# New durations in a schedule planner, constants moved into shared buffers, and 42 slots of SBUF

## The chip, the cores and the metric

The kernel runs on one core of a Trainium2 chip. The metric is the device time of one launch in microseconds; the time before is the median of three runs. TensorE is called PE here, VectorE DVE, ScalarE ACT, GpSimdE POOL, and SyncE SP; SP issues all DMAs of this kernel.

## What is computed

Two layers over 256 tokens of width 1024. Each layer is a gated feed-forward block, a mixer, and another feed-forward block, each with a residual and a layer norm. The mixer of layer 0 joins a gated delta rule (8 heads) with an mLSTM (4 heads); that of layer 1 is a state space mixer (SSD, 32 heads in 4 groups).

```python
def reference(x, ...):
    for l in range(DEPTH):                       # DEPTH = 2
        x = _layer_norm(DN_ALPHA * x + 0.5 * _swiglu(x, ffn_pre_w_gate[l], ffn_pre_w_up[l], ffn_pre_w_down[l]), ...)
        mix = _hybrid_mixer(x, ...) if l % 2 == 0 else _ssd_mixer(x, ...)
        x = _layer_norm(DN_ALPHA * x + mix, ...)
        x = _layer_norm(DN_ALPHA * x + 0.5 * _swiglu(x, ffn_post_w_gate[l], ...), ...)
    return x

def _swiglu(x, w_gate, w_up, w_down):
    return (jax.nn.silu(x @ w_gate) * (x @ w_up)) @ w_down

def _gated_delta_rule(q, k, v, g, beta):         # chunks of the sequence
    ...
    lower = jnp.where(strict, jnp.einsum('bhncd,bhnjd->bhncj', kb, k) * decay, 0.0)
    sol = lax.linalg.triangular_solve(lower + jnp.eye(CHUNK), rhs, left_side=True, lower=True)
    ...
```

## The kernel before, in words

All weights are fp32. A weight tile is loaded in two halves of 512 KB into `raw`; ACT rounds it to `hi`, DVE computes `lo = raw - hi`, and PE multiplies with three products (`mm3`: hi by hi, hi by lo, lo by hi). `wget` keeps `AHEAD` = 4 weights in flight. The feed-forward stages make `gu` (gate and up), then `sg` (Silu on ACT), `hf` (product on DVE), and accumulate the down product in `acc`.

The hybrid mixer (`hyb`) runs token-major products (`tm_chunks`), then the gates of both heads as rows (`softplus`, scans against a tile of ones, a transposition through scratch memory in HBM), the convolutions of k, the matrices `Ls` of the delta rule, and the inverse of its 16 x 16 diagonal blocks (`block_inverse`, all on DVE). The blocks reach the inverse through scratch memory: `Ls` is written to `scrdl`, two loads of 64 KB bring `ab` (pieces of 16 floats), and the results go out through `scrdd` and come back as `T` and `U` for level matmuls of PE. In the meantime the mLSTM part multiplies `mq` and `mk` into `mE`, then `mE` by `mv1`; DVE makes `my` of it, and PE transposes `my`. After it come the convolutions of q and v (`conv_in`: a product in `acc`, ACT's scaled copy `cv` of the PSUM bank, three DVE operations on the same bank, a Silu).

The SSD mixer (`ssd`) has token-major products for `zs`, a softplus and scans, `decays` (a load `abc` of rows from scratch, 8 relus with a bias on ACT and an exponential for each group and half), convolutions for B (`bf`), C (`cf`) and x (`xf`), and `chunk`: `xd`, `xe` and `y` from a transposition, the state `hst` copied by ACT, products `gu`, a normalization, and transpositions into `syh` and `syl`.

The order of the work is not written by hand. Each call is recorded as an `Op` in a `Plan`. `_cost` gives it a duration, `rank` a due time counted backwards from the PE order, and `order` simulates the engines: at each step it takes for each engine the operation with the smallest priority among those that can start (SP and PE never wait for a better one, the others do for a short time), until every queue is fixed. Operations under `hp()` count as 600 places earlier. `behind(op)` says that an operation is placed only after another has been placed. What `order` believes decides only the order; on the chip each engine runs its queue in that order and waits on semaphores. Buffers come from tags with a fixed number of slots (`SB_SLOTS`): `m4` is the large one, for weights and for the mixers' tiles, then `m2`, `m1` and two tiny ones; PSUM has 8 banks. A DMA in the plan ended at max(queue, issue) + bytes/rate + 2000 ns, and 1000 more for `raw`.

Of the kernel before, what the change touches and what calls it, by code (L numbers as in the profile page):

```python
# [19 lines left out]
P = 128  # L20
D = 1024
S = 256
# [10 lines left out]
NSLOT = 40  # L33
# [7 lines left out]
C_EYE16 = 896  # L41
C_LOW16 = 1152
C_N = 1408


def _const_array():
# [9 lines left out]
    c[:, C_LOW16:C_LOW16 + 256] = np.tril(np.ones((16, 16), np.float32), -1).reshape(1, 256)  # L56
    c[:, C_EYE16:C_EYE16 + 256] = np.eye(16, dtype=np.float32).reshape(1, 256)
# [3 lines left out]
SB_SLOTS = {"m4": (NSLOT, WMAX), "m2": (6, 512), "m1": (6, 256), "tiny": (12, 16), "tiny96": (12, 96)}  # L61
# [12 lines left out]
class Buf:  # L74


    def __init__(self, n, tag, shape, dtype, name):
# [6 lines left out]
        self.ops = []  # L84
        self.place = None
# [99 lines left out]
class Plan:  # L185
# [83 lines left out]
    def _cost(self, op, method, a, k):  # L269
# [12 lines left out]
        elif q == "SP":  # L282
# [5 lines left out]
            op.rate = 410 if isinstance(src, bass.AP) and not src.tensor.name.startswith("scr") else 300  # L288
        else:
# [20 lines left out]
            elif q == "ACT":  # L310
                op.busy += 180 + .85 * n + 60 * scal - LAG["ACT"] + (186 if "accum_out" in k else 0)
# [38 lines left out]
    MARGIN, LEAD = 1000, 0  # L350
# [3 lines left out]
    def order(self):  # L354
# [18 lines left out]
        dma = 0.0  # L373
# [12 lines left out]

        def start(o, q):
            t = max(ready[o, q], clock[q])
            if o.news:
# [23 lines left out]
        while len(out) < len(ops):  # L413
            best = None
            for q in QUEUES:
# [4 lines left out]
                now = [(o.prio + 2 * switch(o, q), o.n, t, o) for t, o in can if t <= t0]  # L420
                mine = min(now)
                for p, n, t, o in sorted((o.prio + 2 * switch(o, q), o.n, t, o) for t, o in can if t > t0):

                    if p + self.WAIT * (t - t0) < mine[0] and t - t0 < self.FRAC[q] * mine[3].busy:
                        mine = (p, n, t, o)
                        break
# [20 lines left out]
            if q == "SP":  # L447
                first = max(dma, t + busy)
                dma = first + max(350, o.bytes / o.rate)
                end = dma + 2000 + self.MARGIN * o.raw  # L450
# [6 lines left out]
            o.done, o.begun, o.on = end, t, q  # L457
            out.append(o)
# [32 lines left out]
class Net:  # L491
# [92 lines left out]
    def consts(self):  # L584
# [7 lines left out]
        self.ones = self.one([32, S], F32, name="ones")  # L592
        nc.gpsimd.memset(self.ones, 1.0)
# [277 lines left out]
    def hyb(self, g, b, last=False):  # L871
# [24 lines left out]
        ones = self.ones[0:8]  # L896

# [38 lines left out]
        with hp():  # L936
            sin = t96(12, "sin")
            V.tensor_copy(sin[:, :, 0:8], gt[:, :, 8:16])
            V.tensor_scalar_mul(sin[:, :, 8:12], gt[:, :, 20:24], -1.0)
# [15 lines left out]
            rw = self.m4([8, 4, S], nm="hrows")  # L955
            for half in range(2):
# [130 lines left out]
        mq = self.m4([P, 2, S], nm="mq")  # L1087
# [3 lines left out]
        mk = self.m4([P, 2, S], nm="mk")  # L1091
# [3 lines left out]
        for pr in range(2):  # L1095
            for q in range(2):
# [5 lines left out]
                qk = V.tensor_mul(e, e, ps[:, 0:3 * P])  # L1102
        with hp():
# [533 lines left out]
```

## Time and profile before

| | us |
|---|---|
| median of three runs (1146.54 to 1148.89) | 1147.33 |
| the profiled execution, whole | 1146.67 |
| its span, first to last instruction | 1144.9 |
| PE busy | 1112.7 |
| DVE busy | 758.5 |
| ACT busy | 587.9 |

The mean granted clock of PE is 0.995 of full speed. The feed-forward stages lie at about 0 to 200, 380 to 560, 560 to 750 and 960 to 1145 us, the hybrid mixer at 200 to 380, and the SSD mixer at 750 to 960. Matmuls overlap in PE, so one shows a longer duration (281 ns for 256 columns) than the distance to the next. A row of the list of waits names the waiting engine and tile, the one waited for, us in total, how often, and the longest.

### The profile page before, as it was taken

The page shows a single profiled execution, that of the slowest core. Times are in us where ns is not written, and L with a number is a line of the kernel's source. Part 1 is how long each engine was busy: PE and PEld are TensorE (multiplying, and loading weights), DVE is VectorE, ACT ScalarE, POOL GpSimd, SP SyncE. Part 2 cuts the span into 40 slices and gives each one's busy share as a digit, 9 for nine tenths or more (in the row PEclk, how much of TensorE's full clock was granted, in tenths as well). Part 3 has the DMA queues.
Part 4 walks back from the last instruction along what each step waited for, and adds up shares of the span by engine and source line. Part 5 has one row for each costly group of instructions (what it writes and reads, how often), then busy time and mean ns, then how long its engine had stood idle before and what let it go on. Part 6 is the DMA issues. An engine that isn't in the chain of part 4 may idle for free.

```text
span 1144.9 us, 19783 instructions
## 1 busy us (share of the span) xinstructions
PE 1112.7 (97%) x8118; PEld 1041.5 (91%) x8118; DVE 758.5 (66%) x1242; ACT 587.9 (51%) x890; POOL 26.2 (2%) x53
## 2 busy tenths in 40 slices
PE   7999999998999999999999999999999999999996
PEld 7999998998998999999899999899998779999995
DVE  6945456787969955455865545696788889655425
ACT  6755443593423544344354444379889636444410
POOL 0000000000000000000000000000011220000000
PEclk9999999998999999999999999999999999999999
DMA  9766554648424555565465555465545446655601
GB/s 358 288 212 205 196 183 133 191 171 214 186 102 159 197 190 192 191 206 174 148 223 200 188 197 187 134 217 187 185 146 178 149 163 243 218 172 187 212 19 37
DMA packets 75955, 210.02 MB, mean 183 GB/s; under 512 B 13580, under 2 KB 26328, under 8 KB 75864
## 3 DMA queue, kind: packets, MB, share of 16 engines
q1 hardware_dynamic: 75864, 208.76, 54.3%
q8 instruction: 63, 1.03, 0.4%
q14 instruction: 28, 0.23, 0.1%
HBM read 204.23 MB, written 4.50 MB: 182 GB/s over the span
## 4 chain that ended last, share of the span: by engine, by line
PE 81%; DVE 8%; ACT 6%; DMA 3%; issue 1%; SPq 0%; DVEq 0%; ACTq 0%
PE gu L488 46%; PE acc L488 32%; PE tr L488 3%; DVE cv L488 2%; DMA raw<-in_wgu 2%; DVE lo L488 2%; ACT L488 2%; ACT abc L488 1%; DVE x L488 1%; ACT cv L488 1%; DMA ab<-scrdl 1%; ACT Ls L488 1%; ACT hi L488 0%; DVE ry L488 0%; DMA x<-in_x 0%
## 5 line engine op out<-in xcount | busy, mean ns | idle before, releaser
L488 DVE TENSOR_TENSOR lo<-raw,hi 128x1024 fp32r<-128x1024 f32 (+2 forms) x358 | 428.8, 1216 | 145.0 <-ACT hi L488 141.4
L488 ACT CAST hi<-raw 128x1024 fp32r<-128x1024 f32 (+2 forms) x358 | 370.1, 1045 | 203.0 <-DMA raw<-in_wgu 125.1
L488 PE MATMUL gu<-xl,hi 128*128 128x256 f32 x1216 | 341.9, 281 | 0.0
L488 PE MATMUL gu<-xh,hi 128*128 128x256 f32 x1216 | 341.2, 281 | 0.0
L488 PE MATMUL gu<-xh,lo 128*128 128x256 f32 x1216 | 341.1, 281 | 0.0
L488 PEld LDWEIGHTS gu<-xh,hi 128*128 128x128 f32 x1216 | 229.0, 188 | 1.0
L488 PEld LDWEIGHTS gu<-xl,hi 128*128 128x128 f32 x1216 | 228.9, 188 | 1.1
L488 PEld LDWEIGHTS gu<-xh,lo 128*128 128x128 f32 x1216 | 229.1, 188 | 0.0
L488 PE MATMUL acc<-hi,h 128*128 128x512 f32 (+1 forms) x748 | 228.7, 381 | 0.0
L488 PEld LDWEIGHTS acc<-hi,h 128*128 128x128 f32 x748 | 138.1, 188 | 27.5
L488 PE MATMUL acc<-lo,h 128*128 128x512 f32 (+1 forms) x374 | 142.1, 380 | 0.0
L488 ACT ACTIVATE sg<-gu 128x256 f32<-128x256 f32 (+1 forms) x100 | 35.9, 359 | 183.3 <-PE gu L488 183.1
L488 DVE TENSOR_TENSOR hf<-sg,gu 128x256 f32<-128x256 f32 (+1 forms) x100 | 38.7, 388 | 108.2 <-ACT sg L488 108.0
L488 PE MATMUL acc<-xh,hi 128*128 128x256 f32 x320 | 92.7, 290 | 0.0
L488 PE MATMUL acc<-xl,hi 128*128 128x256 f32 x320 | 90.5, 283 | 0.0
L488 PE MATMUL acc<-xh,lo 128*128 128x256 f32 x320 | 90.2, 282 | 0.0
L488 PEld LDWEIGHTS acc<-lo,h 128*128 128x128 f32 x374 | 70.3, 188 | 13.1
L488 PE MATMUL acc<-hi,xh 128*128 128x260 f32 x224 | 64.0, 286 | 0.0
L488 PE MATMUL acc<-hi,xl 128*128 128x260 f32 x224 | 63.4, 283 | 0.4 <-DVE xl L488 0.4
L488 PE MATMUL acc<-lo,xh 128*128 128x260 f32 x224 | 63.3, 283 | 0.0
L488 PEld LDWEIGHTS acc<-xh,hi 128*128 128x128 f32 x320 | 61.0, 190 | 0.6 <-issue 0.2
L488 DVE TENSOR_TENSOR h<-hf,h 128x256 fp32r<-128x256 f32 x76 | 32.3, 425 | 44.0 <-ACT h L488 44.0
(272 smaller groups left out, 1445.5 us busy)
## 6 DMA issues: line engine op xcount, KB each, us to landing
raw<-in_wgu SPq DMA_DIRECT2D x176, 512.0 KB, 5.0
raw<-in_wd SPq DMA_DIRECT2D x88, 512.0 KB, 5.8
raw<-in_ssd_fm SPq DMA_DIRECT2D x24, 512.0 KB, 5.7
raw<-in_ssd_tm SPq DMA_DIRECT2D x16, 520.0 KB, 4.5
raw<-in_hyb_fm SPq DMA_DIRECT2D x16, 512.0 KB, 5.2
raw<-in_ssd_out SPq DMA_DIRECT2D x16, 512.0 KB, 5.7
raw<-in_hyb_tm SPq DMA_DIRECT2D x12, 520.0 KB, 4.4
raw<-in_hyb_out SPq DMA_DIRECT2D x8, 512.0 KB, 6.8
```

Source lines behind the costliest of these rows:

```text
L488: getattr(engines[o.on], method)(*map(real, a), **{x: real(v) for x, v in k.items()})
```

## The change

The planner's numbers: a DMA that reads or writes scratch memory in pieces of up to 64 bytes counts 82 bytes/ns, other scratch writes 228 and reads 291 (300 before); DMAs end at the later of issue + 2100 + bytes/rate and the end of the one before + bytes/rate, with 1300 ns more for the second large one of a row, and `LATE` = 200 on top; `MARGIN`, now used by `rank` alone, is 1500. An operation that touches a PSUM bank starts in the plan only when every other engine's last operation on that bank has ended. An ACT operation with a per-partition scalar that reads no PSUM counts 40 ns more. The switching penalty gets a name, `SWITCH` = 2, its value before.

Memory: `m4` has 42 slots instead of 40. The 16 x 16 constants leave `cst` (1408 to 896 columns) for an input of their own, `cst16`, that is loaded into an `m2` slot (`c16`) behind the last `qk`. The tile of ones, set once at the start, becomes two `m1` tiles, set on POOL behind `neg` in the hybrid mixer and behind `soft` in the SSD mixer. `mq` and `mk` share one `m4` slot. `tiny96` has 11 slots of 64.

```diff
@@ -30,7 +30,7 @@
...
 WMAX = KB * CW
-NSLOT = 40
+NSLOT = 42
 RSQRT_MAGIC = 0x5F3759DF
@@ -38,9 +38,7 @@
...
 C_PAIR = 768
-C_EYE16 = 896
-C_LOW16 = 1152
-C_N = 1408
+C_N = 896
@@ -53,12 +51,16 @@
...
     c[:, C_CAU:C_CAU + P] = i <= j
-    c[:, C_LOW16:C_LOW16 + 256] = np.tril(np.ones((16, 16), np.float32), -1).reshape(1, 256)
-    c[:, C_EYE16:C_EYE16 + 256] = np.eye(16, dtype=np.float32).reshape(1, 256)
     return c
...
-SB_SLOTS = {"m4": (NSLOT, WMAX), "m2": (6, 512), "m1": (6, 256), "tiny": (12, 16), "tiny96": (12, 96)}
+def _const16():
+
+    c = np.stack([np.eye(16, dtype=np.float32), np.tril(np.ones((16, 16), np.float32), -1)])
+    return np.broadcast_to(c.reshape(1, 512), (P, 512)).copy()
+
+
+SB_SLOTS = {"m4": (NSLOT, WMAX), "m2": (6, 512), "m1": (6, 256), "tiny": (12, 16), "tiny96": (11, 64)}
 PS_SLOTS = {"ps": 8}
@@ -82,6 +84,7 @@
...
         self.ops = []
+        self.seen = {}
         self.place = None
@@ -285,7 +288,10 @@
...
             op.raw = "raw" in getattr(getattr(out, "buf", None), "name", "")
-            op.rate = 410 if isinstance(src, bass.AP) and not src.tensor.name.startswith("scr") else 300
+            far = [v for v in (out, src) if isinstance(v, bass.AP)][0]
+            if far.tensor.name.startswith("scr"):
+                piece = 4 * far.ap[-1][1]
+                op.rate = 82 if piece <= 64 else 228 if isinstance(src, View) else 291
         else:
@@ -308,7 +314,7 @@
...
             elif q == "ACT":
-                op.busy += 180 + .85 * n + 60 * scal - LAG["ACT"] + (186 if "accum_out" in k else 0)
+                op.busy += 180 + .85 * n + 60 * scal - LAG["ACT"] + (40 if scal and not ps else 0) + (186 if "accum_out" in k else 0)
                 f = a[2] if method == "activation" and len(a) > 2 else None
@@ -347,7 +353,8 @@
...
     PE_DUE = False
-    MARGIN, LEAD = 1000, 0
+    SWITCH = 2
+    MARGIN, LATE, LEAD = 1500, 200, 0
     WAIT = 2
@@ -370,7 +377,7 @@
...
         clock["SP"] = 700.0
-        dma = 0.0
+        dma, row = 0.0, 0
         table = None
@@ -384,8 +391,17 @@
...
+        for o in ops:
+            o.banks = list({v.buf for _, a, k in o.calls for v in list(a) + list(k.values())
+                            if isinstance(v, View) and v.buf.psum})
+
         def start(o, q):
             t = max(ready[o, q], clock[q])
+            for b in o.banks:
+
+                for e, end in b.seen.items():
+                    if e != q:
+                        t = max(t, end + HAND[e][q])
             if o.news:
@@ -417,9 +433,9 @@
...
                 t0 = max(min(t for t, _ in can), clock[q] + 1)
-                now = [(o.prio + 2 * switch(o, q), o.n, t, o) for t, o in can if t <= t0]
+                now = [(o.prio + self.SWITCH * switch(o, q), o.n, t, o) for t, o in can if t <= t0]
                 mine = min(now)
-                for p, n, t, o in sorted((o.prio + 2 * switch(o, q), o.n, t, o) for t, o in can if t > t0):
+                for p, n, t, o in sorted((o.prio + self.SWITCH * switch(o, q), o.n, t, o) for t, o in can if t > t0):
@@ -445,9 +461,10 @@
...
             if q == "SP":
-                first = max(dma, t + busy)
-                dma = first + max(350, o.bytes / o.rate)
-                end = dma + 2000 + self.MARGIN * o.raw
+                took = max(350, o.bytes / o.rate)
+                row = 1 if t + busy >= dma else row + 1
+                dma = max(t + busy + 2100 + took, dma + took + (1300 if row == 2 and took > 900 else 0))
+                end = dma + self.LATE
             if q == "ACT" and o.exps is not None:
@@ -455,6 +472,8 @@
...
             o.done, o.begun, o.on = end, t, q
+            for b in o.banks:
+                b.seen[q] = end
             out.append(o)
@@ -589,8 +608,6 @@
...
         self.x = self.one([P, 2, D], F32, name="x")
-        self.ones = self.one([32, S], F32, name="ones")
-        nc.gpsimd.memset(self.ones, 1.0)
         self.mhalf = self.one([P, 1], F32, name="mhalf")
@@ -893,8 +910,6 @@
...
             DQ(al, self.ap["gdn_a_log"].partition_broadcast(P))
-        ones = self.ones[0:8]
-
         gt = self.one([P, 2, 24], F32, name="hgate")
@@ -936,7 +951,7 @@
...
             V.tensor_copy(sin[:, :, 0:8], gt[:, :, 8:16])
-            V.tensor_scalar_mul(sin[:, :, 8:12], gt[:, :, 20:24], -1.0)
+            neg = V.tensor_scalar_mul(sin[:, :, 8:12], gt[:, :, 20:24], -1.0)
             beta = t96(8, "beta")
@@ -953,6 +968,9 @@
...
             rw = self.m4([8, 4, S], nm="hrows")
+            ones = self.m1([8, S], nm="ones")
+            with self.plan.behind(neg):
+                G.memset(ones, 1.0)
             for half in range(2):
@@ -1084,11 +1102,12 @@
...
-        mq = self.m4([P, 2, S], nm="mq")
+        mqk = self.m4([P, 4, S], nm="mqk")
+        mq = mqk[:, 0:2]
         ps = self.acc()
...
         A.copy(flat(mq), ps)
-        mk = self.m4([P, 2, S], nm="mk")
+        mk = mqk[:, 2:4]
         ps = self.acc()
@@ -1100,8 +1119,11 @@
...
                 qk = V.tensor_mul(e, e, ps[:, 0:3 * P])
+        c16 = self.m2([P, 512], nm="c16")
+        with self.plan.behind(qk):
+            DQ(c16, self.ap["cst16"])
         with hp():
-            self.block_inverse(ab, c, dd)
+            self.block_inverse(ab, c16, dd)
         lazy["sg"] = sg = self.m4([P, 2, 512], nm="sg")
@@ -1285,8 +1307,8 @@
...
         ti = self.m1([P, 16, 16], nm="ti")
-        eye3 = c[:, C_EYE16:C_EYE16 + 256].rearrange("p (a b) -> p a b", a=16)
-        V.tensor_mul(ab, ab, c[:, C_LOW16:C_LOW16 + 256].rearrange("p (a b) -> p a b", a=16))
+        eye3 = c[:, 0:256].rearrange("p (a b) -> p a b", a=16)
+        V.tensor_mul(ab, ab, c[:, 256:512].rearrange("p (a b) -> p a b", a=16))
         V.tensor_sub(an, eye3, ab)
@@ -1362,7 +1384,6 @@
...
             DQ(vec, self.ap["ssd_vec"].partition_broadcast(P))
-        ones = self.ones[:, 0:P]
         t32 = lambda n, nm: self.one([P, n, NH], F32, name=nm)
@@ -1388,7 +1409,7 @@
...
         sp = self.softplus(flat(sdt), 2 * NH)
-        V.tensor_copy(flat(dt), sp)
+        soft = V.tensor_copy(flat(dt), sp)
         nega = t32(1, "snega")
@@ -1397,6 +1418,9 @@
...
         rw = self.m1([NH, S], nm="srow")
+        ones = self.m1([NH, P], nm="ones")
+        with self.plan.behind(soft):
+            G.memset(ones, 1.0)
         ds_ = [self.scratch([NH, P], f"ds{half}") for half in range(2)]
@@ -1574,7 +1598,7 @@
...
     f = lambda a: np.ascontiguousarray(np.asarray(a))
-    o = {"cst": _const_array(), "ident": np.eye(P, dtype=np.float32), "x": f(i["x"])[0]}
+    o = {"cst": _const_array(), "cst16": _const16(), "ident": np.eye(P, dtype=np.float32), "x": f(i["x"])[0]}
     gu, dn = [], []
```

## Rows read from the trace of the kernel before

**Rows 1.** The page's part 1: busy us, share of the span, instructions.

```profile
PE 1112.7 (97%) x8118; PEld 1041.5 (91%) x8118; DVE 758.5 (66%) x1242; ACT 587.9 (51%) x890; POOL 26.2 (2%) x53
```

**Rows 2.** Whom PE waited for: us in total, times, longest us.

```profile
PE tr L488 <- DMA x<-in_x: 5.2, 1, 5.2
PE tr L488 <- DVE my L488: 4.5, 1, 4.5
PE gu L488 <- DVE xe L488: 2.7, 2, 1.7
PE gu L488 <- ACT hst L488: 2.7, 3, 1.9
PE tr L488 <- ACT cf L488: 1.8, 2, 1.5
```

**Rows 3.** One window of 20 us: length, busy us by engine, granted clock, DMA.

```profile
860.00:880.00 20.00, 18.49 (x144) 17.15 (x144) 17.23 (x27) 18.62 (x29) 4.23 (x10) 1.00 0.42 143
```

**Rows 4.** Windows of 2 us around PE's longest stall.

```profile
274.00:276.00 2.00, 2.00 (x10) 2.00 (x11) 1.17 (x7) 0.00 (x0) 0.00 (x0) 0.50 0.85 90
276.00:278.00 2.00, 2.00 (x11) 2.00 (x10) 1.22 (x6) 0.59 (x1) 0.00 (x0) 0.50 0.83 209
278.00:280.00 2.00, 2.00 (x16) 2.00 (x14) 1.97 (x5) 0.00 (x0) 0.00 (x0) 0.71 1.15 327
```

**Rows 5.** Timeline of PE: start, us, what, count [idle before and releaser].

```profile
267.47 1.95 PE L488 MATMUL tr<-mv,mE 128*128 128x129 f32 x16
273.91 0.45 PE L488 MATMUL tr<-ident,my 128*128 128x128 f32 x1 [4.49 <-DVE my L488]
...
301.09 1.05 PE L488 MATMUL gu<-U,Ls 128*128 128x128 f32 x8
```

**Rows 6.** Timeline of DVE in the hybrid mixer.

```profile
259.66 2.35 DVE L488 TENSOR_TENSOR lo<-raw,hi 128x1024 fp32r<-128x1024 f32 x2
264.26 0.43 DVE L488 TENSOR_TENSOR ab<-ab,cst 128x256 f32<-128x256 f32 x1 [2.25 <-DMA ab<-scrdl]
...
273.41 0.61 DVE L488 SCALAR_TENSOR_TENSOR my<-tr,md,sg 128x128 f32<-128x128 f32 x2
```

**Rows 7.** Timeline of SP's DMA issues in the hybrid mixer.

```profile
256.45 0.73 SPq L488 DMA_DIRECT2D ab<-scrdl  x1
...
277.85 1.48 SPq L488 DMA_DIRECT2D T<-scrdd  x1
```

**Rows 8.** DMA issues: count, KB each, median us from issue to landing.

```profile
raw<-in_wgu SPq DMA_DIRECT2D x176, 512.0 KB, 5.0
...
T<-scrdd SPq DMA_DIRECT2D x2, 512.0 KB, 8.3
...
snw<-in_ssd_norm_w SPq DMA_DIRECT2D x4, 256.0 KB, 3.9
...
ab<-scrdl SPq DMA_DIRECT2D x2, 64.0 KB, 6.4
```

**Rows 9.** Chain that ended last: start, us, what.

```profile
40.81 11.37 PE gu L488 x96
```

**Rows 10.** Timelines of ACT and DVE at one convolution of the SSD mixer.

```profile
790.33 0.55 ACT L488 ACTIVATE cv<-acc,scw 128x256 f32<-128x256 f32 x1
...
790.91 0.48 DVE L488 SCALAR_TENSOR_TENSOR cv<-acc,scw,cv 128x255 f32<-128x255 f32 x1 [2.19 <-ACT cv L488]
```

**Rows 11.** Groups of ACT by shape: count, busy us, mean ns.

```profile
L488 ACT ACT_TABLE_LOAD x38 | 48.8, 1283 | 3.4 <-DVE cv L488 2.1 <-PEq L1626 0.7
...
L488 ACT ACTIVATE abc<-abc,spam 128x128 f32<-128x128 f32 x64 | 20.2, 392 | 0.7 <-DVE sde L488 0.7
```

**Rows 12.** Timelines of ACT and PE at a stall in the SSD mixer.

```profile
832.16 1.06 ACT L488 ACTIVATE abc<-abc 128x1024 f32<-128x1024 f32 x1
833.12 0.57 ACT L488 COPY hst<-gu 128x512 f32<-128x512 f32 x1
...
833.74 1.12 PE L488 MATMUL gu<-hst,cf 128*128 128x512 f32 x2 [1.92 <-ACT hst L488]
```

## The prediction

> **What bounds the kernel now.** I read the engine totals first, then who TensorE (PE) waited for, then the same waits by stretch. PE is busy 97% of the span, 1112.7 us of 1144.9 [rows 1]; no instruction of PE is removed by the change, so it can win only among the 32.2 us in which PE stands still, and in time in which PE runs at the lower clock. The waits of PE show where the idle time lies [rows 2]: 5.2 us for the first load of x, which nothing can hide, and then single stalls in the two mixers: 4.5 us for `my` in the hybrid mixer, and 2.7 (`xe`), 2.7 (`hst`) and 1.8 us (`cf`) in the SSD mixer, 7.2 us together. The reader is to see that each of them is one to three places, and that, behind the first load, none of these is a load of weights. A window of 20 us from the SSD mixer shows the other kind [rows 3]: PE loses 1.5 us at full clock, beside an ACT that is busy for 18.6 of 20 us.
>
> The largest stall costs more than its length. Behind it, in pieces of 2 us [rows 4], the granted clock is 0.50 for 4 us (the level of 1.2 GHz) and 0.71 over the next two, in which it comes back to 2.4: 2 x 0.5 + 2 x 0.5 + 2 x 0.29 = 2.6 us lost on top of 4.5. So this one place costs 7.1 us, 0.6% of the kernel. The 1.5 us that PE loses in rows 3 leave the clock at 1.00.
>
> **Why it stalls.** The order is made by `Plan.order`, which guesses when each operation ends and then fixes every queue. PE finishes `tr<-mv,mE` at about 269.4 (267.47 + 1.95) and next has `tr<-ident,my`, which begins at 273.91 [rows 5]. On DVE [rows 6] the load `ab<-scrdl` makes the block inverse start at 264.26, after DVE had been free since 262.01 (259.66 + 2.35); the inverse runs from there with `my` queued behind it, which begins at 273.41. The second `ab` load is issued at 256.45 [rows 7] and is awaited until 264.26, 7.8 us; the median of both is 6.4 us [rows 8]. The plan of before gives such a load 0.33 us of issue, 0.35 of transfer and 2.0 of latency, 2.7 us, so it expects the inverse, and `my`, far too early. Meanwhile `lo` of the next two weights is done at 262.01, so PE could have run the q convolution's 96 matmuls; 96 matmuls take 11.37 us [rows 9], more than twice the stall.
>
> **The change part by part.**
> 1. *Rates of small loads.* `op.rate` falls from 300 to 82 bytes/ns for pieces of up to 64 bytes, so each 64 KB `ab` load now takes 0.80 instead of 0.35 us in the plan. The write of `Ls` (512 byte pieces) goes from 1.75 to 2.30 us each, and the second of a row gets 1.3 us more. Following the plan's own formula along the queue (two `Ls` writes, three weight loads of 1.28 us, two `ab` loads) the second `ab` comes some 2.2 us later in the plan than it did. These are the plan's beliefs, used for the order alone, and not times of the kernel. If `my` comes 2.2 us later there, PE finds other ready matmuls first: at 11.37/96 = 0.118 us each and groups of six, about three groups. At the least 2.2 us of the stall goes and, if the 2.3 us that remain leave the clock alone, as the 1.5 us in rows 3 do, the clock's 2.6 us too: 4.8 us. At the most the whole 7.1 goes. The correction is made in the plan alone, so DVE is not faster; PE's later users of `my` are the output products far behind. I take 6.0.
>
>    A page speaks against this term: the Trainium skill, "DMA: Bandwidth & Descriptors", section "Anatomy of one DMA", gives about 2.0 us fixed plus bytes over 436 GB/s; that is 2.15 us (an estimate from this page) for 64 KB, near the old plan, and by it the correction would be wrong and the term nothing. The trace has 6.4 us for the load, and the measurement decides.
>
> 2. *One reader per PSUM bank.* The plan now lets no second engine at a bank before the first is done. The trace has that order already [rows 10]: ACT reads a bank from 790.33 to 790.88, and DVE, which needs `cv` of it, begins at 790.91 after 2.19 us without work. One pair of rows cannot show the bank alone as the cause. The rule removes nothing from the chip; it makes the convolutions of the plan longer, so that PE is given other work ahead of their consumers (`cf`, 1.8 us).
>
> 3. *Relu with bias.* The plan counts 40 ns more for each of the 64 `abc` relus, 2.6 us of ACT's work in the SSD mixer, and 16 in the hybrid; the trace has 392 ns for one [rows 11], where the old formula says 349. Parts 2 and 3 aim at `hst`, `xe` and `cf`. `hst` is put in ACT's queue behind an exponential at 832.16 and begins at 833.12; PE's `gu<-hst` follows at 833.74 [rows 12]. These stalls come from an ACT that is nearly full there, not from one wrong number, so later guesses cure only those for which PE has other work. Bounds: all 7.2 us gained, or as much lost if the new order makes them worse. I take a quarter, 1.8, nearest to the `cf` stall, the one that hangs on the convolution itself.
>
> 4. *Loads of weights.* The plan now lands a lone 512 KB load 0.7 us sooner and wants it 0.5 us earlier (MARGIN 1500), and there are 42 slots, less one slot in the hybrid since `mq` and `mk` share one. A `wgu` load takes 5.0 us from issue to landing in the trace, with what is queued ahead of it [rows 8], where the plan now has 0.33 + 1.28 + 2.1 + 0.2 = 3.9 for a lone one. PE waits for no load of weights, so nothing is gained; what hides the 1.1 us of difference is the four weights that `wget` keeps ahead. If that cover were gone, 1.1 us would be lost at each of six stage starts, 6.6 us. I take 0.
>
> 5. *Constants.* `cst` shrinks by 256 KB and `c16` brings 256 KB: bytes are the same, one DMA is added. `c16` is queued on SP behind the last product with `mE`, so it comes out near the `ab` loads, and the block inverse waits for both. Its nearest row is `snw`, 256 KB, 3.9 us to landing [rows 8], shorter than `ab`'s 6.4; but the weight loads queued behind it on SP come one issue later (0.4 to 0.7 us), and its data takes part of `ab`'s bandwidth. So the inverse may start 0 to 2 us later. What waits for the inverse is the scratch copy into `T` and `U`: the second `T` is issued at 277.85 [rows 7] with a landing of 8.3 us [rows 8], so about 286, and PE's first product with `U` begins at 301.09 [rows 5]: cover of some 15 us. While `my` stands behind the inverse, though, 2 us would go into the stall. I take 0.5 against the change.
>
> 6. *Memsets.* The 1.0s are set on POOL in the mixers, 256 and 128 columns each; POOL is busy 2% [rows 1]. They stand behind `neg` and `soft` in the plan, and DVE's scans wait for them; what hides them is the softplus on DVE between. POOL's 53 instructions take 0.5 us on the mean (26.2/53). I take nothing; 0.5 us each if uncovered. The `ones` memset at the start goes: nothing, as x's load is awaited.
>
> Sum: -6.0 - 1.8 + 0.5 = -7.3 us. Against the profiled execution's 1146.67 (its span and 1.8 us around it) that is 1139.4; the median shown is 0.7 us above that execution, so 1140.1, and I write 1140.0.
>
> **The rivals.**
> - *The stall stays in place.* The plan's `my` moves, but not beyond the end of `tr<-mv,mE`, or the inverse goes first once more. Then 7.1 us stay, parts 2 and 3 bring 1.8 and part 5 takes 0 to 2: 1145.5 to 1147.5. For it: PE takes the oldest ready operation, and `my` is older than the q convolution. Against: 96 matmuls are ready, and 2.2 us is many groups.
> - *A new stall in the SSD mixer, slower.* There ACT does table loads of 1.28 us for single short operations (38 in all, 48.8 us [rows 11]). If the new order puts one more pair of them and an exponential, 2 x 1.28 + 1.06 = 3.6 us, ahead of `hst` in two of the four groups, the stall of 1.9 becomes 5.5 us, above the 4.5 us that brought the lower clock, with 2.6 us more: 2 x (3.6 + 2.6) = 12.4. With the gain of 6 that is 1147.3 - 6 + 12.4 = 1153.7. It decides from a stall of about 4.5 us. For it: ACT is 93% busy in 860:880. Against: the plan now counts ACT's work more nearly as it is, and the penalty on switching is unchanged.
> - *More goes.* All of the 7.1 and two thirds of the 7.2: 1147.3 - 7.1 - 4.8 = 1135.4.
>
> **How the numbers follow.** Forecast 0.50, more goes 0.19, stall stays 0.15, new stall 0.16. About 0.2% (2.3 us) is what a measurement of this kernel can tell from no change: below 1145.0 is faster, above 1149.6 slower. The forecast and the better case give faster 0.69 and the new stall 0.16; what is left, 0.15, is the same. The range reaches from 1132 (nearly all of 7.1 and 7.2 gained, which would be 1133, and 1 us for the scatter) to 1149 (the stall in place with the 2 us of part 5, 1147.5, and a late memset and a late load, 0.5 + 1.1), and leaves out the slower case.
>
> **What the profile would show.** Right: PE's longest wait after the first load is below 2.5 us; no piece of the hybrid mixer shows a granted clock under 0.9; `acc<-xh,hi` stands ahead of the last `tr<-ident,my`. Part 3 right: the waits for `hst`, `xe` and `cf` sum to about 5.4 us. Wrong: a wait of over 4 us on `hst` or `xe`, more than 38 table loads, or `ab` and `c16` landing after 266 with `my` behind them.

## The result, and the profile after

The changed kernel takes 1133.98 us in the median of four runs (1133.38 to 1135.16) against 1147.77 us of the kernel before on the same chip: a ratio of 0.9881 with a 95% interval of [0.9864, 0.9898], so 13.7 us faster (11.7 to 15.6). The forecast was 1140.0 us with a range of 1132 to 1149. The sign held and the time is in the range, but the gain is nearly twice the 7.3 us of the sum and is nearest to the rival "more goes" (1135.4).

The profiled execution of the changed kernel took 1135.16 us, its span is 1133.4, so the two profiled executions differ by 11.5 us. PE's busy time has hardly moved [rows 1]; the page's part 1:

```profile
PE 1109.6 (98%) x8118; PEld 1039.1 (92%) x8118; DVE 757.2 (67%) x1242; ACT 585.9 (52%) x886; POOL 24.0 (2%) x54
```

Whom PE waited for in the changed kernel (us in total, times, longest):

```profile
PE tr L507 <- DMA x<-in_x: 5.0, 2, 4.7
PE gu L507 <- DVE xe L507: 2.7, 3, 1.2
...
PE tr L507 <- DVE y L507: 1.0, 1, 1.0
PE tr L507 <- DVE my L507: 0.7, 1, 0.7
```

Against [rows 2], `my` fell from 4.5 to 0.7 us, `hst` and `cf` are gone from the list, and `xe` is the same in sum, in more and shorter pieces.

Where the time went is read best by stage. I cut both traces at the last `xl` of each layer norm (at 208.2, 378.2, 567.7, 755.4, 957.0 us before and 208.6, 371.5, 561.1, 748.4, 945.3 us after) and let the trace sum each stretch. The windows of the hybrid mixer and of the SSD mixer, first the kernel before (length, busy us of PE, PEld, DVE, ACT, POOL, granted clock, DMA share, GB/s):

```profile
208.20:378.20 170.00, 163.23 (x1299) 152.53 (x1298) 139.92 (x348) 86.13 (x143) 0.00 (x0) 0.98 0.51 166
755.40:957.00 201.60, 193.62 (x1403) 178.64 (x1402) 163.52 (x268) 154.85 (x262) 23.36 (x40) 1.00 0.53 179
```

and then the changed kernel:

```profile
208.60:371.50 162.90, 160.08 (x1297) 149.82 (x1296) 137.65 (x347) 86.84 (x143) 0.00 (x0) 1.00 0.55 174
748.40:945.30 196.90, 192.98 (x1403) 178.41 (x1402) 163.87 (x268) 152.16 (x260) 20.97 (x40) 1.00 0.54 183
```

The hybrid mixer is 7.1 us shorter: PE's idle time fell from 6.77 to 2.82 us (length less busy), and its busy time by 3.15 us, because the granted clock rose from 0.98 to 1.00. The SSD mixer is 4.7 us shorter, nearly all of it idle time, 7.98 to 3.92 us. The four feed-forward stages changed by at most 0.4 us each. The two mixers, 11.8 us, are the whole difference of the two executions; the 2 us more of the comparison lie in the scatter of the runs: the profiled execution of the kernel before is near the lower end of its four (1146.54 to 1148.89), that of the changed kernel is the slowest of its four.

The place of the largest stall, PE of the changed kernel (start, us, what, count, idle before and releaser):

```profile
267.92 2.84 PE L507 MATMUL tr<-mv,mE 128*128 128x129 f32 x24
270.51 0.37 PE L507 MATMUL acc<-xh,hi 128*128 128x256 f32 x1
...
272.20 1.21 PE L507 MATMUL tr<-ident,my 128*128 128x128 f32 x4 [0.73 <-DVE my L507]
```

All 24 products with `mE` and one group of the q convolution now stand ahead of the first `my`, where [rows 5] had 16, and every window of 2 us from 262 to 282 shows a clock of 1.00, where [rows 4] had 0.50 and 0.71; one of them:

```profile
274.00:276.00 2.00, 2.00 (x20) 2.00 (x19) 1.89 (x7) 0.04 (x1) 0.00 (x0) 1.00 0.91 154
```

DVE there:

```profile
259.02 2.35 DVE L507 TENSOR_TENSOR lo<-raw,hi 128x1024 fp32r<-128x1024 f32 x2
261.50 1.22 DVE L507 TENSOR_TENSOR lo<-raw,hi 128x1024 fp32r<-128x1024 f32 x1
262.63 0.42 DVE L507 TENSOR_TENSOR ab<-ab,c 128x256 f32<-128x256 f32 x1
...
271.70 0.61 DVE L507 SCALAR_TENSOR_TENSOR my<-tr,md,sg 128x128 f32<-128x128 f32 x2
```

The inverse begins at 262.63 without a wait for `ab`, 1.6 us earlier than in [rows 6], where DVE stood still for 2.25 us; here DVE makes another half weight's `lo` before it. So PE's wait for `my` fell by 3.8 us in two ways: the work that PE has ahead of it ends 2.05 us later (271.47 against 269.42), and `my` comes 1.7 us earlier (272.20 against 273.91). On SP the writes of `Ls` go out 1.2 us earlier than before and the second `ab` 0.7 us earlier than in [rows 7]; `c16` (here `c`) stands between the two `ab`. The write before the change, and then the changed kernel:

```profile
250.62 2.44 SPq L488 DMA_DIRECT2D scrdl<-Ls  x2
```

```profile
249.44 2.44 SPq L507 DMA_DIRECT2D scrdl<-Ls  x2
...
252.64 1.06 SPq L507 DMA_DIRECT2D ab<-scrdl  x1
253.76 0.81 SPq L507 DMA_DIRECT2D c<-in_cst  x1
...
255.75 0.59 SPq L507 DMA_DIRECT2D ab<-scrdl  x1
```

### The profile page after: what moved, and what is told of

Read it like the earlier page. It is cut to its first block, busy times and chain, and to the rows that moved or that the text cites. A ratio compares the mean times of both kernels' runs of the same rounds, so it can differ in the third digit from the quotient of the medians.

```text
span 1133.4 us, 19825 instructions
## 1 busy us (share of the span) xinstructions
PE 1109.6 (98%) x8118; PEld 1039.1 (92%) x8118; DVE 757.2 (67%) x1242; ACT 585.9 (52%) x886; POOL 24.0 (2%) x54
## 4 chain that ended last, share of the span: by engine, by line
PE 85%; DVE 6%; DMA 3%; ACT 3%; issue 1%; SPq 0%; DVEq 0%; ACTq 0%
PE gu L507 47%; PE acc L507 35%; PE tr L507 3%; DVE lo L507 1%; DVE cv L507 1%; DVE x L507 1%; ACT abc L507 1%; DMA raw<-in_wd 1%; DMA raw<-in_hyb_out 1%; DMA x<-in_x 1%; DMA raw<-in_wgu 1%; ACT L507 1%; DMA raw<-in_ssd_fm 0%; ACT cv L507 0%; SPq L507 0%
## 5 line engine op out<-in xcount | busy, mean ns | idle before, releaser
L507 PEld LDWEIGHTS acc<-xl,hi 128*128 128x128 f32 x320 | 60.4, 189 | 0.0
```

The lines of the kernel that those rows point to most:

```text
L507: getattr(engines[o.on], method)(*map(real, a), **{x: real(v) for x, v in k.items()})
```

## Experiments

Each kernel ran beside the kernel before on the same chip. "Gain" is one less the ratio, times about 1148 us; `my` is PE's wait for it in the one profiled execution. The rows come from more than one chip, so compare ratios rather than medians.

| kernel | median us | ratio, 95% interval | gain us | `my` us |
|---|---|---|---|---|
| changed | 1133.98 | 0.9881 [0.9864, 0.9898] | 13.7 | 0.7 |
| before, PE's queue alone rearranged | 1146.78 | 0.9988 [0.9977, 1.0000] | 1.4 | 1.6 |
| before + rates | 1145.83 | 0.9991 [0.9975, 1.0007] | 1.0 | 3.2 |
| before + end of a DMA, MARGIN | 1147.06 | 0.9990 [0.9976, 1.0005] | 1.1 | 4.7 |
| before + bank rule | 1141.28 | 0.9952 [0.9934, 0.9969] | 5.5 | 5.1 |
| before + all numbers | 1140.34 | 0.9917 [0.9895, 0.9940] | 9.5 | 1.6 |
| before + memory, 40 slots | 1149.66 | 1.0004 [0.9983, 1.0026] | -0.5 | 4.4 |
| changed, 40 slots | 1135.53 | 0.9877 [0.9855, 0.9899] | 14.1 | 1.9 |
| changed, without bank rule | 1142.17 | 0.9947 [0.9929, 0.9965] | 6.1 | 2.8 |
| memory, 40 slots, PE's queue rearranged | 1153.00 | 1.0041 [1.0025, 1.0057] | -4.7 | 1.2 |
| before, groundless nudge | 1150.22 | 1.0019 [1.0006, 1.0032] | -2.2 | 3.9 |
| changed, 40 slots, groundless nudge | 1141.87 | 0.9958 [0.9942, 0.9973] | 4.8 | 0.9 |
| changed, 40 slots, old DMA numbers | 1146.12 | 0.9979 [0.9967, 0.9991] | 2.4 | 4.9 |

### The stall alone: PE's queue rearranged

The plan of before is left as it is; afterwards eight groups of the first q convolution are put ahead of the first transposition of `my` in PE's queue.

```diff
+    AHEAD_OF_MY = 8
...
+        first = next(n for n, o in enumerate(order) if o.on == "PE" and tile(o)[:2] == ["tr", "my"])
+        bank = next(o.calls[0][1][0].buf for o in order[first:] if o.on == "PE" and tile(o)[0] == "acc")
+        moved = [o for o in order[first:] if o.on == "PE" and o.calls[0][1][0].buf is bank][:self.AHEAD_OF_MY]
...
+        rest = [o for o in order[first:] if o not in set(moved)]
+        return order[:first] + moved + rest
...
         order = self.order()
+        order = self.ahead_of_my(order)
```

> The kernel before with its plan unchanged; afterwards 8 groups of 6 matmuls of the first q convolution are put, in PE's queue alone, ahead of the first transposition of `my`. Every other queue keeps its order. My price for the stall, if it is the stall: the 48 matmuls take 5.7 us at 0.118 us each, longer than the 4.5 us of waiting, so the wait for `my` goes and the granted clock stays at 1.00 in 272 to 280: 7.1 us less than before, 1140.7, and nothing changes in the SSD mixer. Rival, that the stall is covered by something that comes next (ACT and DVE then wait for `my` longer and hand the loss on to the q convolution): the wait reappears behind, and the time falls by 4.5 us or less.

It gained 1.4 us, not 7, and its interval ends at no change; the rival holds. The lower clock did go (1.00 from 260 to 280 us) and the wait for `my` fell from 4.5 to 1.6 us, but a new wait came. PE's:

```profile
PE tr L506 <- ACT qf L506: 2.1, 2, 1.7
...
PE tr L506 <- DVE my L506: 1.6, 1, 1.6
```

and behind them DVE is full, while PE has time to spare (windows of 5 us):

```profile
285.00:290.00 5.00, 4.50 (x37) 4.12 (x36) 5.00 (x8) 2.41 (x5) 0.00 (x0) 1.00 1.07 342
290.00:295.00 5.00, 3.35 (x28) 2.98 (x27) 5.00 (x9) 4.71 (x8) 0.00 (x0) 1.00 0.97 365
```

PE did the q convolution earlier, but what comes after it goes at the pace of the other queues, which were not touched. Covering a stall on PE alone hands it on.

### The numbers one at a time, and together

The first kernel has the rates alone:

```diff
-            op.rate = 410 if isinstance(src, bass.AP) and not src.tensor.name.startswith("scr") else 300
...
+            if far.tensor.name.startswith("scr"):
+                piece = 4 * far.ap[-1][1]
+                op.rate = 82 if piece <= 64 else 228 if isinstance(src, View) else 291
```

> The kernel before with the new rates of scratch transfers alone (82, 228 and 291 bytes/ns). If the price of the small `ab` loads is what moved `my`: the wait for `my` falls below 2 us and the clock stays up, some 5 to 7 us less, 1140.5 to 1142.5, and the SSD mixer keeps its 201 us within 1. Rival, that any new number reshuffles the plan: the SSD mixer moves by 2 us or more though no rate that matters there changed, and the wait for `my` need not be the one that goes.

The next has the new end of a DMA with MARGIN 1500 alone:

```diff
-    MARGIN, LEAD = 1000, 0
+    MARGIN, LATE, LEAD = 1500, 200, 0
...
-                end = dma + 2000 + self.MARGIN * o.raw
...
+                dma = max(t + busy + 2100 + took, dma + took + (1300 if row == 2 and took > 900 else 0))
+                end = dma + self.LATE
```

> The kernel before with the new end of a DMA alone (issue + 2100 + transfer, 1300 for the second of a row, 200, MARGIN 1500), the old rates. If the rates are what counts for `ab`, the wait for `my` stays above 3 us and the time within 2 us of before. If the rhythm of the loads counts too (the two writes of `Ls` in a row now end later), the wait falls as with the rates, 1140 to 1143. Reshuffling: the SSD mixer moves by 2 us or more either way.

The next has the bank rule alone:

```diff
+            for b in o.banks:
...
+                for e, end in b.seen.items():
+                    if e != q:
+                        t = max(t, end + HAND[e][q])
...
```

> The kernel before with the rule of one reader per PSUM bank alone. By my reasons: the hybrid mixer keeps its wait for `my` (4 to 5 us) and the SSD mixer gets shorter, as `cf` and `hst` are planned later: 1 to 4 us less, 1143.5 to 1146.5. Reshuffling: the wait for `my` changes by over 2 us although the rule says nothing of `ab`, and the SSD mixer may get longer.

And the last has these three and the 40 ns of the relu, with the old memory; of its diff the part on the relu:

```diff
-                op.busy += 180 + .85 * n + 60 * scal - LAG["ACT"] + (186 if "accum_out" in k else 0)
+                op.busy += 180 + .85 * n + 60 * scal - LAG["ACT"] + (40 if scal and not ps else 0) + (186 if "accum_out" in k else 0)
```

> The kernel before with all four corrections of the plan's numbers (rates, end of a DMA, banks, relu), and its memory as it was: 40 slots, constants and ones at their old places, no `c16`. If the numbers carry the gain, as I forecast: 1133 to 1137, as the changed kernel. If memory and numbers are needed together, or if the result is a shuffle of the plan: somewhere between 1137 and 1148, with stalls at other places than in the changed kernel.

The first two cannot be told from no change, the bank rule gains 5.5 us, all together 9.5. All together miss the 1133 to 1137 of the expectation. PE's waits with the rates alone, and two rows of PE's timeline:

```profile
PE tr L491 <- DVE my L491: 3.2, 1, 3.2
PE tr L491 <- DVE ri L491: 2.9, 1, 2.9
```

```profile
268.64 2.84 PE L491 MATMUL tr<-mv,mE 128*128 128x129 f32 x24
...
275.38 0.30 PE L491 MATMUL tr<-ident,my 128*128 128x128 f32 x1 [3.19 <-DVE my L491]
```

The rates do act on the stall, from 4.5 to 3.2 us, but `ri`, a wait in the layer norm behind the mixer that is not on the list of before, takes it back: the hybrid mixer and the feed-forward stage behind it take 359.7 us together, 359.5 before. What the rates alone did gain lies in the SSD mixer, 197.8 us against 201.6, with no wait for `hst`; their rival, that any new number reshuffles the plan, said so. The kernel with all numbers has `my` at 1.6 and the same `ri` at 2.8 us. The end of a DMA alone leaves `my` at 4.7 us, and its SSD mixer is 204.5 us long, at a clock of 0.98, so its rival holds too. It does change the stall: the inverse begins at 262.74, but DVE makes the `lo` of two halves (2.35 us) between it and `my`.

The bank rule alone gained more than the 1 to 4 us expected. Its profiled execution took 1146.06 us, 4.8 above its median, at a mean clock of 0.988, where five of its nine executions had 0.996 or 0.997; so its stages are not compared. In that execution `my` is still awaited, 5.1 us, as expected.

### The memory alone, 40 slots, and the changed kernel without the bank rule

The changed memory (`c16`, `ones` set on POOL, `mq` and `mk` in one slot, `tiny96`) with 40 slots and the old numbers; of its diff the part on `c16`:

```diff
+        c16 = self.m2([P, 512], nm="c16")
+        with self.plan.behind(qk):
+            DQ(c16, self.ap["cst16"])
...
```

> The changed kernel's memory moves alone (`c16`, two tiles of ones, `mq` and `mk` in one slot, smaller `tiny96`) with 40 slots and all of the plan's old numbers. My forecast had 0 to 2 us of loss here: 1147 to 1149. If a shuffle of the plan is what counts, it moves by 3 us or more to either side, and the second `ab` load has other loads ahead of it than before.

Nothing is gained (0.5 us slower, and the interval holds no change), though the inverse starts as early as in the changed kernel, at 262.97 us:

```profile
262.97 0.41 DVE L498 TENSOR_TENSOR ab<-ab,c 128x256 f32<-128x256 f32 x1
```

PE still waits 4.4 us for `my`, at the lower clock (0.83 from 260 to 280; the profiled execution is 2.8 us above the median). DVE does the `lo` of two halves of a weight between the inverse and `my`:

```profile
271.23 2.35 DVE L498 TENSOR_TENSOR lo<-raw,hi 128x1024 fp32r<-128x1024 f32 x2
```

So an earlier inverse does not remove the stall by itself.

The changed kernel with 40 slots:

```diff
-NSLOT = 42
+NSLOT = 40
```

> The changed kernel with 40 slots instead of 42. I gave the slots nothing: within 1 us of the changed kernel, 1133 to 1135. If the slots carry the gain: 1140 or more. If a shuffle: 2 to 8 us more, and from stalls that have no load of weights in them.

The two slots bring nothing: 0.9877 and 0.9881 lie in each other's intervals. This kernel stands for the changed one where an edit needs the room of a slot. It also shows how little the stall says by itself: PE waits 1.9 us for `my`, and the clock falls behind it,

```profile
274.00:276.00 2.00, 2.00 (x11) 2.00 (x10) 1.84 (x9) 0.59 (x1) 0.00 (x0) 0.50 0.92 169
276.00:278.00 2.00, 2.00 (x16) 2.00 (x15) 1.39 (x2) 0.00 (x0) 0.00 (x0) 0.74 0.75 209
```

yet the hybrid mixer takes 163.0 us, as against 162.9 with 42 slots, where the wait is 0.7 us and the clock stays at 1.00.

The changed kernel without the bank rule:

```diff
-            for b in o.banks:
...
-                for e, end in b.seen.items():
-                    if e != q:
-                        t = max(t, end + HAND[e][q])
```

> The changed kernel without the rule of one reader per bank. The rule alone gave 5.5 us on the kernel before. If it works by itself and adds up: 1139 to 1140, and the loss lies in the SSD mixer. If parts do not add up: anything from 1134 to 1146, with part of the loss in the hybrid mixer.

Without the bank rule 7.6 us of the 13.7 go (0.9947 against 0.9881), and both mixers lose, as the second of the two expectations had it. The stages say where: the hybrid mixer takes 167.7 us (162.9 in the changed kernel) with 2.8 us of wait for `my`, the SSD mixer 201.7 (196.9). In the SSD mixer a wait of 2.2 us for `xe` brings the lower clock (windows of 2 us; the clock is the third number from the end):

```profile
880.00:882.00 2.00, 0.13 (x2) 0.00 (x0) 2.00 (x3) 1.97 (x3) 0.00 (x0) 1.00 0.00 0
882.00:884.00 2.00, 1.69 (x4) 0.79 (x4) 1.90 (x3) 1.97 (x3) 0.00 (x0) 0.66 0.00 0
884.00:886.00 2.00, 2.00 (x12) 2.00 (x11) 1.29 (x2) 2.00 (x5) 0.00 (x0) 0.50 0.00 0
...
888.00:890.00 2.00, 2.00 (x6) 1.05 (x6) 1.97 (x4) 0.00 (x0) 0.00 (x0) 0.63 0.00 0
```

The window left out shows 0.50, so that is 2 x (0.34 + 0.50 + 0.50 + 0.37) = 3.4 us of clock on top of the 2.2, more than the 4.8 us by which the stage is longer.

### An early inverse and a rearranged PE queue together

The kernel with the memory alone, with the rearranged queue of the first experiment on top.

```diff
+        order = self.ahead_of_my(order)
```

> The kernel with the changed memory, the old numbers and 40 slots (no visible gain by itself, 1149.66 us), with one more edit behind the planning: in PE's queue eight groups of the first q convolution go ahead of the first transposition of my. So the block inverse starts early (262.97 without a wait for ab) and PE has other work during it. Theory A (DVE sets the pace from 260 to 300, and its order is not touched): PE's wait for my goes and the clock stays at 1.00 from 260 to 280, but the time comes back as waits for qf or for my a few us later; the hybrid mixer gains at most 2 us, 1147.5 to 1150. Theory B (an early inverse and matmuls for PE are together enough for the gain of the mixer): 5 to 7 us below the kernel with the memory alone, 1142.5 to 1145, no new PE wait above 1.5 us in the hybrid mixer. Nothing of the computation is left out.

It is 4.7 us slower than before: theory B fell. Theory A was right in what comes (the wait for `my` falls to 1.2 us, the clock is 1.00 from 260 to 280, the time comes back as a wait for `qf`) and wrong in the size, above its 1150, and in the engine. PE's new wait:

```profile
PE tr L516 <- ACT qf L516: 5.9, 2, 4.4
```

ACT's timeline shows what it hangs on, and it is not the DVE that theory A had named (DVE itself waits 3.22 us for ACT's `cv` there):

```profile
289.35 1.05 ACT L516 CAST hi<-raw 128x1024 fp32r<-128x1024 f32 x1 [3.03 <-DMA raw<-in_hyb_out]
290.30 0.83 ACT L516 ACTIVATE cv<-acc,hcw 128x256 f32<-128x256 f32 x2
...
293.66 0.72 ACT L516 ACTIVATE qf<-cv 128x256 f32<-128x256 f32 x2
```

ACT's queue has a weight's rounding, which waits 3.03 us for its load, ahead of the convolution's `cv`, and `qf` comes after. PE has done the convolution long before; ACT's fixed order keeps it waiting. A queue that is rearranged alone meets the order of the others.

### How much a groundless nudge moves

One number of the planner is moved with no reason from a trace, the hand-over from DVE to DVE, first in the kernel before, then in the changed one with 40 slots.

```diff
-        "DVE": {"PE": 55, "DVE": 35, "ACT": 35, "POOL": 89, "SP": 60},
+        "DVE": {"PE": 55, "DVE": 45, "ACT": 35, "POOL": 89, "SP": 60},
```

> The kernel before with one number of the planner moved for no reason that a trace gives: the hand-over from DVE to DVE is 45 ns instead of 35. It reorders about as many places of the queues as one of the real corrections does. Theory (the corrections work through what they say, the bank rule above all): the time stays within 2.5 us of the kernel before, 1145 to 1150.5, with a PE wait of 4 to 5 us for my and a lower clock at 260 to 280. Rival (any reordering moves the few stalls about by several us, and the corrections are lucky draws): 4 us or more off the kernel before, to either side. Nothing of the computation is left out.

2.2 us slower, inside the theory's 2.5. The wait for `my` stays (3.9 us), and waits in the layer norms come: `x` 3.3 us in three places, `xl` 2.0.

> The changed kernel with 40 slots (1135.53 us) and the same groundless nudge: hand-over from DVE to DVE 45 ns instead of 35. Theory (the corrected numbers make the order robust): within 2.5 us of 1135.5, 1133 to 1138, and no PE wait above 2 us behind the first load. Rival (lucky draw): it falls back by 4 us or more towards the kernel before, 1139.5 to 1145, with a stall of 2 us or more for my, ri, xe or hst. Nothing of the computation is left out.

The rival holds here: 9.3 us of the 14.1 are lost by the ratios (6.3 between the medians, 5.4 between the two profiled executions). Yet not where the prediction looked: `my` is 0.9 us, the clock is 1.00 from 260 to 280, and the hybrid mixer with the stage behind it is as long as without the nudge (352.2 and 352.1 us). The loss is at layer norms, 2.9 us of it in the feed-forward stage ahead of the SSD mixer (191.3 us against 188.4), and in the SSD mixer (198.6 us against 195.8):

```profile
PE tr L507 <- DVE x L507: 3.3, 3, 2.2
...
PE gu L507 <- DVE xl L507: 2.4, 2, 2.0
```

So the gain in the hybrid mixer survived this nudge, and about half of that in the SSD mixer. In the kernel before, the nudge took 2.6 us off the same two stages (356.9 us against 359.5), so of two nudged kernels the changed one is 4.7 us shorter there.

### The changed kernel with the old DMA numbers

Memory, bank rule and relu stay; rates, end of a DMA and MARGIN are the old ones; 40 slots.

```diff
...
-                op.rate = 82 if piece <= 64 else 228 if isinstance(src, View) else 291
+            op.rate = 410 if isinstance(src, bass.AP) and not src.tensor.name.startswith("scr") else 300
...
-    MARGIN, LATE, LEAD = 1500, 200, 0
+    MARGIN, LATE, LEAD = 1000, 200, 0
...
-                end = dma + self.LATE
...
+                end = dma + 2000 + self.MARGIN * o.raw
```

> The changed kernel with 40 slots, with the old rates, the old end of a DMA and MARGIN 1000: the memory moves, the bank rule and the relu term stay. Theory of the prediction (the rates of the small loads carry the 6 us of the stall for my): 1140.5 to 1142.5, PE waits 4 us or more for my and the clock is below 0.9 at 260 to 280. Rival (the bank rule with the memory moves carries it, the DMA numbers bring the 1 to 2 us that they bring alone): 1136 to 1138.5, the wait for my below 2.5 us, clock 1.00 at 260 to 280. Nothing of the computation is left out.

11.7 us of the 14.1 go (10.6 between the medians); 1146.12 us is above the theory's 1140.5 to 1142.5. The stall is back in full, as the theory said, with a clock of 0.83 from 260 to 280; PE's timeline:

```profile
266.90 2.17 PE L503 MATMUL tr<-mv,mE 128*128 128x129 f32 x18
274.00 0.45 PE L503 MATMUL tr<-ident,my 128*128 128x128 f32 x1 [4.93 <-DVE my L503]
```

and DVE's, where a half's `lo` stands between the inverse and `my`, which begins at 273.51; in the changed kernel, with 42 slots and with 40, none stands there:

```profile
262.20 1.22 DVE L503 TENSOR_TENSOR lo<-raw,hi 128x1024 fp32r<-128x1024 f32 x1
263.33 0.42 DVE L503 TENSOR_TENSOR ab<-ab,c 128x256 f32<-128x256 f32 x1
...
271.58 1.22 DVE L503 TENSOR_TENSOR lo<-raw,hi 128x1024 fp32r<-128x1024 f32 x1
```

The stage windows of the two mixers:

```profile
208.50:378.30 169.80, 163.43 (x1301) 153.02 (x1300) 140.38 (x349) 86.26 (x143) 0.00 (x0) 0.98 0.53 168
...
755.20:956.40 201.20, 196.98 (x1412) 182.78 (x1412) 163.71 (x269) 152.68 (x262) 21.12 (x40) 0.98 0.53 179
```

The hybrid mixer is 169.8 us long, as before the change (170.0) and 6.8 more than with the new DMA numbers. The SSD mixer loses 5.5 us, which neither the prediction nor the expectation had. The same windows of the changed kernel with 40 slots:

```profile
209.00:372.00 163.00, 159.96 (x1297) 150.81 (x1296) 138.44 (x348) 88.40 (x144) 0.00 (x0) 0.99 0.54 175
...
750.20:945.90 195.70, 192.48 (x1395) 177.89 (x1395) 162.13 (x268) 152.62 (x260) 24.52 (x40) 1.00 0.54 183
```

Most of the loss in the SSD mixer comes from a small wait in a bad place. DVE's timeline with the old DMA numbers:

```profile
829.39 1.23 DVE L503 TENSOR_TENSOR lo<-raw,hi 128x1024 fp32r<-128x1024 f32 x1 [1.83 <-ACT hi L503]
830.53 0.69 DVE L503 TENSOR_TENSOR xd<-tr,sdt 128x512 f32<-128x512 f32 x1
```

PE's:

```profile
828.20 1.89 PE L503 MATMUL gu<-xd,abc 128*128 128x64 f32 x16
831.36 1.07 PE L503 MATMUL gu<-xd,abc 128*128 128x64 f32 x8 [1.27 <-DVE xd L503]
```

and the windows behind it:

```profile
832.00:834.00 2.00, 2.00 (x6) 1.04 (x6) 2.00 (x3) 1.14 (x2) 0.00 (x0) 0.58 0.00 0
834.00:836.00 2.00, 2.00 (x11) 1.93 (x10) 0.36 (x2) 1.69 (x4) 0.75 (x2) 0.50 0.00 0
```

`xd` stands in DVE's queue behind the `lo` of a weight that waits 1.83 us for ACT; PE stands still for 1.27 us between narrow products, and the clock falls. It is 0.58, 0.50, 0.50 and 0.71 over four windows: 2 x (0.42 + 0.50 + 0.50 + 0.29) = 3.4 us, more than twice the stall itself.

## Why the prediction was right in sign and short in size

*Part 1, the rates (taken at 6.0, bounds 4.8 to 7.1).* The size came out: with everything else in place the DMA numbers are worth 6.8 us in the hybrid mixer, and in the changed kernel the signs named are there (no single wait of PE above 1.3 us behind the first load; no lower clock at the stall's place; q convolution ahead of the last `my`). But the signs do not carry the size: with 40 slots the clock falls to 0.50 behind a wait of 1.9 us and the gain is the same. What failed is the working. I priced the stall by itself, as if PE's time there were the time of the kernel. The rearranged queue removed the clock loss and most of the wait and gained 1.4 us, and with the early inverse it lost 4.7. In the kernels that I tried, the 6 to 7 us come only when the whole plan moves, with the loads, DVE's `lo` and ACT's casts in the same order as PE's work. The term also missed what the DMA numbers do in the SSD mixer, 5.5 us.

The way was another one as well. "About three groups" of the q convolution were to fill the stall; one did, with 42 slots, and none with 40. The rest of the 2.05 us by which PE's work ends later are the eight other products with `mE` and a later start, and 1.7 us come from an earlier `my`, which the prediction had not counted on ("DVE is not faster"). Nor is it the rates alone. With them alone PE has the same 24 products ahead of the first `my` as in the changed kernel, but the inverse begins late, at 265.74. The earlier `Ls` go with the end of a DMA and MARGIN: counted from the start of the last `xl` ahead of the mixer, the writes go out at 40.5 to 41.3 us in the five kernels that have it and at 42.8 to 42.9 us in the seven that have not, the two nudged ones left aside. How much each of the two is worth is not shown. That the term came out at its size is thus in part luck.

The page that spoke against this term, the Trainium skill's "DMA: Bandwidth & Descriptors", section "Anatomy of one DMA — SWDGE (gpsimd) path", gives its figure for a DMA on the GpSimd path. Here SP issues the load, behind loads of weights, and the trace does not have the estimate of 2.15 us: the median of `ab` from issue to landing is 6.4 us before and still 5.9 us in the changed kernel. Taking the DMA numbers back costs 11.7 us.

*Parts 2 and 3, bank rule and relu (taken at 1.8, bounds 7.2 either way).* This is the mis-sized term, as far as its stage goes. The SSD mixer gained 4.7 us, `hst` and `cf` went altogether, and `xe` stayed at 2.7; forecast were 5.4 us for the three, found 2.7. "Later guesses cure only those for which PE has other work" undervalued how much is ready. But the 4.7 us are not the rule's alone: they go without the bank rule (201.7 us) and they go without the DMA numbers (201.2), and the rates alone bring 3.8 (197.8). And I looked for the rule in the SSD mixer alone, while taking it out costs 4.8 us in the hybrid mixer as well, which has convolutions of the same form. Alone it gains 5.5 us, taken out of the changed kernel it costs 7.6: the same sign twice. But the groundless nudge costs as much, so that this is the rule's mechanism and not in part a lucky order is not shown. DVE's wait for `cv` in the SSD mixer fell from 11.0 us in 12 places to 8.2 in 9, which fits it. The relu was not tried alone, so no run shows its share.

*Part 4, slots and loads (0).* Right: 40 slots gain 14.1 us, 42 gain 13.7.

*Part 5, constants (0.5 against).* The direction was wrong. `c16` is loaded between the two `ab` loads, and the inverse begins 1.6 us earlier, not 0 to 2 later; with the memory alone it is 1.3 us earlier (262.97 against 264.26). By itself that is worth nothing (the memory alone is 0.5 us slower, and its interval holds no change).

*Part 6, memsets (0).* Right: no wait of PE or of DVE for POOL shows in the changed kernel.

*The sum.* The parts do not add. Rates 1.0, DMA formula 1.1, bank rule 5.5 and memory -0.5 make 7.1 by themselves, uncertain by some 4 us (an estimate from the four intervals); together they make 13.7 (the relu is not in this sum). Taken out one at a time, the DMA numbers cost 11.7 and the bank rule 7.6. Two things make this so: a stall that goes in one place comes out in the next (`ri`, `qf`), and a stall of 1.3 us or more brought 1.5 to 3.4 us of lower clock, or none, so that a small shift can count double. Between the kernel with all numbers and the changed one, 4.2 us (0.9917 to 0.9881) are open: the former has the `ri` wait of 2.8 us and a clock of 0.91 from 360 to 380 (20 x 0.09 = 1.8 us), which would make it up, but the memory alone has `ri` too, so that the memory moves remove it is not shown.

*The rivals.* "More goes" was the nearest, with 7.1 us in the hybrid mixer, as it said, and 4.7 against 4.8 us in the SSD mixer. It rests on the same account of the stall as the sum, so that it came so near is partly luck. "The stall stays" is what happens without the DMA numbers. "A new stall in the SSD mixer" did not come: the table loads fell from 38 to 34. But it was put off for the wrong reason. Its threshold, a stall of about 4.5 us, is not what it took: the clock fell behind 2.2 us in one kernel and behind 1.27 in another.

## What to carry to other kernels

Price a stall by what all engines' queues do behind it, not by its length: where PE alone was covered and the loads and casts behind it kept their order, the stall moved on, twice. In a list scheduler correct the durations as a set and measure the set; single corrections, each right by the trace, can show nothing. And nudge the tuned version with a number that means nothing: here one nudge cost 5 to 9 us of 14.1, which says how much of a gain can hang on the order's luck, and which part of it (the hybrid mixer's) held. It is one draw; whether another nudge would spare the same part is not shown.

## What was not expected of the hardware

The granted clock fell to 0.50 behind an idle time of PE of 1.27 us (834 to 838 us, old DMA numbers) and of 2.2 us (884 to 888 us, no bank rule), while 1.5 us in 20 left it at 1.00 in [rows 3], and the kernel with all numbers waited 1.6 us for `my` with the clock at 1.00 from 260 to 280. In the first case PE had done narrow products, 16 of 64 columns, just before and went on with 8 more of them and two of 512 columns. In the second it had done eight transpositions of 128 columns and went on with 512 and then 64 columns. The length of the stall alone does not decide; what does was not settled here.

At one and the same place, the wait for `my`, the loss does go with the length. Behind waits of 0.7 to 1.6 us (five kernels) the clock is 1.00 from 260 to 280. Behind 1.9 to 3.9 us (four) the windows of 2 us add up to 1.5 to 1.7 us lost, behind 4.4 to 5.1 us (five, the kernel before among them) to 2.1 to 2.7 us. These are fourteen single executions at one place, and no rule.

Nor does a kernel's order fix the loss. The nine executions of the kernel with the bank rule alone took 1139.89 to 1146.56 us, and the two above 1146 us are the two at a mean granted clock of 0.988; the others had 0.993 to 0.997.
